# Linear layer with bias and residual on one core: the weight in one load behind the bias, and the last two x loads moved forward in the queue

## Chip, core and metric

The kernel runs on one core of one Trainium2 chip. The metric is device time in microseconds (us). The core's compute engines are called by their short names: PE is TensorE, DVE is VectorE, ACT is ScalarE, POOL is GpSimd. SP is SyncE, which computes nothing here and only issues transfers (DMAs).

## The reference

All arrays are float32.

```python
batch, m, k, n = 16, 512, 1024, 768   # x: batch,m,k  weight: k,n  bias: n  residual, out: batch,m,n
def reference(x, weight, bias, residual):
    return (np.matmul(x, weight) + bias + residual).astype(np.float32)
```

In and out this is 33.6 MB of x, 3.1 MB of weight, 25.2 MB of residual and 25.2 MB of output, 87.05 MB in all.

## The kernel before

x is taken as 8192 rows, split into 8 groups of 1024 rows. A group is 8 tiles of 128 rows, and it is worked on in two halves of 4 tiles. Every partition holds 8 consecutive rows of a group, so a load of a whole group of x moves 32 KB in one piece for each partition, a load of half a group 16 KB, and a residual or an output group 24 KB.

**The engines.** For each half, ACT casts x to bf16 in two steps (L131, semaphore `cast`, 4 casts a group). DVE transposes blocks of 32 x 32 (L161 and L167), and ACT moves half of the transposed blocks to their places (L136). PE multiplies: 64 matmuls for a half (L327), into four buffers in PSUM (`po`). DVE adds the residual while it takes the result out of PSUM (`evacuate`, L173, semaphore `ev`), two tiles at a time, in place in the residual's buffer. POOL adds the bias to the same two tiles (`add_bias`, L222, semaphore `add`), and from there they are stored. The second pair of evacuations of a group stands behind the transposes of the next group's first half on DVE.

At the start POOL casts the weight to bf16 in two halves (L217, semaphore `wc`); PE waits for both (L314). DVE clears `bias_rows` (L175), waits for the bias, and spreads it over all partitions with a shuffle (L178), all of it ahead of its first transposes.

**The buffers.** One array `data` holds everything that is transferred: four slots for residuals (`r_home`, group g in slot g % 4) and two for x (`x_home`: even groups at X0, odd ones at X1). The weight is staged in the slot of residual 3. The residual of group 7 has no slot of its own; it goes where x of group 6 was.

**The queue.** Every DMA is issued by SP, from one list, `ORDER`, written by hand. `x3` is the load of x of group 3, `x0a` and `x0b` are the halves of group 0, `w0` and `w1` the halves of the weight, `r3` the residual of group 3, `st3` the store of group 3, `st4+` the store of groups 4 and 5 in one DMA, `st7a` to `st7c` the store of group 7 in three parts. SP goes through the list in order and, ahead of each DMA, waits for what that DMA needs. A wait holds all that stands behind it in the list:

- an x load of group g > 1 waits until the group two earlier is cast (`cast`, L260);
- `r4`, `r5` and `r6` wait until the store that last used their slot has landed (L275); `r7` waits until x of group 6 is cast (L271);
- a store waits until the bias has been added to its last tiles (L286);
- the bias load waits until DVE has cleared `bias_rows` (L251);
- every load waits for the load before it on the same semaphore to have landed. This is the helper `load_into`:

```python
before = landed.get(name, 0)
landed[name] = before + 16
if before:
    wait(sp, name, before)
```

The residuals r0 to r7 share the semaphore `r`. Whole x loads and first halves share `xa`, second halves share `xb`; for whole loads SP raises `xb` itself (L264 and L273), by an amount that it works out from `ORDER`.

Of the kernel before, what the change touches and what calls it, by code (L numbers as in the profile page):

```python
# [13 lines left out]
G = 8  # L14
B = 4

ORDER = ("x0a w0 bias w1 x0b r0 x1a x1b r1 x2 r2 x3 r3 x4 st0 "
         "st1 r4 x5 r5 st2 x6a x6b r6 x7 r7 st3 st4+ st6 st7a st7b st7c").split()
PARTS = {"": (0, 8), "a": (0, 4), "b": (4, 8)}
LAST_PARTS = {"a": (0, 3), "b": (3, 6), "c": (6, 8)}  # L20
SPLIT = "st7a"
# [3 lines left out]
def shares(name):  # L25
    if name != SPLIT:
        return [slice(0, P)]
    return [slice(APART, P)] + [slice(m, APART, STEP) for m in range(STEP)]


@with_exitstack
def kernel(
    ctx: ExitStack,
    tc: tile.TileContext,
    x: bass.AP,
    weight: bass.AP,
    bias: bass.AP,
    residual: bass.AP,
    out: bass.AP,
):  # L40
    nc = tc.nc
    stored = ctx.enter_context(nc.semaphore("st"))
    late = 16 * sum(len(shares(name)) for name in ORDER if name[:2] == "st" and int(name[2]) > 2)
    nc.scalar.sem_inc(stored, late)
    with tc.tile_critical(name="all", no_gpsimd_drain=True):  # L45
        emit(nc, ctx, x, weight, bias, residual, out, stored, late)
    nc.sync.wait_ge(stored, late)


def emit(nc, es, x, weight, bias, residual, out, stored, late):  # L50
# [5 lines left out]
    R = K // P  # L56
# [5 lines left out]
    sp, act, dve, pool, pe = nc.sync, nc.scalar, nc.vector, nc.gpsimd, nc.tensor  # L62
# [18 lines left out]
    def sem(name):  # L81
        if name not in sems:
            sems[name] = es.enter_context(nc.semaphore(name))
        return sems[name]

    def wait(eng, name, value):
        eng.wait_ge(sem(name), value)  # L87
# [14 lines left out]
    def group(ap, g):  # L102
        return ap[g * G * P:(g + 1) * G * P, :].rearrange("(p j) k -> p j k", p=P)

    def span(start, size):
        return data[:, start:start + size] if isinstance(start, int) else data[:, bass.ds(start, size)]

    def x_home(g):
        return X0 - (g % 2) * X_SLOT

    def x_rows(start, j, n):
        return span(start + j * K, n * K).rearrange("p (t k) -> p t k", k=K)

    def r_home(g):

        return (g % 4) * R_SLOT + ((g + 1) // n_grp) * (X0 - 3 * R_SLOT)

    def r_rows(start, j, n):
        return span(start + j * N, n * N).rearrange("p (j n) -> p j n", n=N)

    w_stage = span(3 * R_SLOT, R * N).rearrange("p (r n) -> p r n", n=N)
    w_rows = weight.rearrange("(p r) n -> p r n", p=P)
# [90 lines left out]

    for h in (0, 1):
        part = slice(h * (R // 2), (h + 1) * (R // 2))
        wait(pool, f"w{h}", 16)
        pool.tensor_copy(out=w_sb[:, part, :], in_=w_stage[:, part, :]).then_inc(sem("wc"), 1)  # L217
    wait(pool, "bb", 1)

# [20 lines left out]
    def load_into(name):  # L240
# [5 lines that stand above are left out]
        return name  # L246

    for name in ORDER:
        into = name
        if name == "bias":  # L250
            wait(sp, "ev", EV0)  # L251
            src, dst = bias[None, :].to_broadcast((P // Q, N)), bias_rows[0:P:Q, :]
        elif name[0] == "w":
            k0 = int(name[1]) * (R // 2)
            src, dst = w_rows[:, k0:k0 + R // 2, :], w_stage[:, k0:k0 + R // 2, :]
        elif name[0] == "x":
            g, part = int(name[1]), name[2:]
            j0, j1 = PARTS[part]
            if g > 1 and part != "b":
                wait(sp, "cast", 2 * (2 * g - 2))  # L260
            if g == 3:
                wait(sp, "wc", 2)
                whole = 16 * sum(n[0] == "x" and len(n) == 2 and int(n[1]) < n_grp - 1 for n in ORDER)
                sp.sem_inc(sem("xb"), whole)  # L264
                landed["xb"] += whole
            into = load_into("xb" if part == "b" else "xa")
            src, dst = group(x2d, g)[:, j0:j1, :], x_rows(x_home(g), j0, j1 - j0)
        elif name[0] == "r":
            g = int(name[1])
            if g == n_grp - 1:  # L270
                wait(sp, "cast", 2 * (2 * g))  # L271
                if f"x{g}" in ORDER:
                    sp.sem_inc(sem("xb"), 16)  # L273
            elif g > 3:
                wait(sp, f"st{g - 4}", 16)  # L275
            into = load_into("r")
            src, dst = group(res2d, g), r_rows(r_home(g), 0, G)
        else:
            g, part = int(name[2]), name[3:]
            n = 2 if part == "+" else 1  # L280
            j0, j1 = (LAST_PARTS if g == n_grp - 1 else PARTS)[part.strip("+")]
            end = (g + n - 1) * G + j1
            if end == n_sub:
                wait(sp, "ev", ev_end)
            else:
                wait(sp, "add", added[(end - 1) | 1])  # L286
            src, dst = r_rows(r_home(g), j0, j1 - j0), group(out2d, g)[:, j0:j1, :]
            if n > 1:
                src = span(r_home(g), n * R_SLOT).rearrange("p (g k) -> p g k", g=n)
                dst = out2d[g * G * P:(g + n) * G * P, :].rearrange(  # L290
                    "(g p j) n -> p g (j n)", g=n, p=P)
            if g > 2:
                into = "st"
        for rows in shares(name):
            sp.dma_start(out=dst[rows] if name == SPLIT else dst,  # L295
                         in_=src[rows] if name == SPLIT else src).then_inc(sem(into), 16)
# [20 lines left out]
    with pe.Fori(0, n_bat):  # L317
        tiles = iter(range(B))
        for i in range(B):
# [5 lines left out]
            for k in range(R):  # L325
                for c, (n0, nl) in enumerate(chunks):
                    ins = pe.add_instruction(mybir.InstMatmult(  # L327
                        name=nc.get_next_instruction_name(),
# [36 lines left out]
```

## Time and profile before

| | before |
|---|---|
| time, median of 3 runs | 209.27 us (209.25 to 209.3) |
| profiled execution | 209.01 us |
| its span, first to last instruction | 207.2 us |
| mean granted PE clock | 0.984 |
| busy: PE, DVE, ACT, POOL | 170.6, 166.3, 144.9, 115.5 us |
| DMA queue, share of 16 engines' span | 98.3% |
| bytes read, written | 61.88 MB, 25.17 MB |
| SP waiting on landed x, residuals, stores | 51.9, 50.8, 24.4 us |

The profile is of one execution. Busy time is that of instructions with work in them; issuing a DMA and waiting count as idle. A DMA has an issue, which takes SP about 0.33 us, and a landing, which is when its semaphore is full. In between it may stand in the queue behind others. Between the span and the time of the profiled execution lie 1.8 us in which nothing of the kernel runs.

### The profile page before, as it was taken

The page shows a single profiled execution, that of the slowest core. Times are in us where ns is not written, and L with a number is a line of the kernel's source. Part 1 is how long each engine was busy: PE and PEld are TensorE (multiplying, and loading weights), DVE is VectorE, ACT ScalarE, POOL GpSimd, SP SyncE. Part 2 cuts the span into 40 slices and gives each one's busy share as a digit, 9 for nine tenths or more (in the row PEclk, how much of TensorE's full clock was granted, in tenths as well). Part 3 has the DMA queues.
Part 4 walks back from the last instruction along what each step waited for, and adds up shares of the span by engine and source line. Part 5 has one row for each costly group of instructions (what it writes and reads, how often), then busy time and mean ns, then how long its engine had stood idle before and what let it go on. Part 6 is the DMA issues. An engine that isn't in the chain of part 4 may idle for free.

```text
span 207.2 us, 2315 instructions
## 1 busy us (share of the span) xinstructions
PE 170.6 (82%) x1024; PEld 50.6 (24%) x512; DVE 166.3 (80%) x180; ACT 144.9 (70%) x162; POOL 115.5 (56%) x38
## 2 busy tenths in 40 slices
PE   0000999989998999999999999699999999999900
PEld 0000222323332333233332322133322222233200
DVE  1068496999889989999899978998999899983510
ACT  2357976997599696979697679888797969730000
POOL 0055007639391939193938484484829391999800
PEclk9999999999999999999999999999999999999985
DMA  6999999999999999999999999999999999999995
GB/s 209 429 431 436 446 427 414 433 433 487 411 405 449 411 455 405 419 441 455 408 427 474 411 427 413 429 440 449 408 465 411 446 399 441 455 408 427 451 399 218
DMA packets 4472, 87.05 MB, mean 420 GB/s; under 512 B 500, under 2 KB 500, under 8 KB 632
## 3 DMA queue, kind: packets, MB, share of 16 engines
q1 hardware_dynamic: 4472, 87.05, 98.3%
HBM read 61.88 MB, written 25.17 MB: 420 GB/s over the span
## 4 chain that ended last, share of the span: by engine, by line
DMA 77%; PE 10%; DVE 4%; issue 2%; ACT 1%; SPq 0%; DVEq 0%; ACTq 0%
DMA data<-in_x_dram 66%; DMA out_dram<-data 12%; PE po L327 10%; DVE xt L167 2%; DVE data L173 1%; ACT xb L131 1%; DVE tq L161 1%; SPq L295 0%; DVEq L98 0%; SPq L87 0%; ACTq L98 0%; SPq L360 0%; SPq L45 0%
## 5 line engine op out<-in xcount | busy, mean ns | idle before, releaser
L327 PE MATMUL po<-w_sb,xt 128*128 128x512 bf16 (+1 forms) x1024 | 170.6, 329 | 25.9 <-DVE xt L167 20.5
L222 POOL TENSOR_TENSOR data<-data,bias_bc 128x1536 f32<-128x1536 f32 x32 | 109.8, 3455 | 68.3 <-DVE data L173 68.2
L136 ACT COPY xt<-tq 32x512 uint32<-32x512 uint32 x128 | 78.9, 617 | 21.3 <-DVE tq L161 18.5
L167 DVE STREAM_TRANSPOSE xt<-xb 32x512 uint32<-32x512 uint32 x128 | 90.1, 704 | 3.9 <-ACT xb L131 1.9
L327 PEld LDWEIGHTS po<-w_sb,xt 128*128 x512 | 50.6, 99 | 145.5 <-issue 143.9
L131 ACT CAST xb<-data 128x2048 bf16 x32 | 64.8, 2076 | 16.1 <-DMA data<-in_x_dram 15.8
L173 DVE TENSOR_TENSOR data<-po,data 128x1536 f32 (+2 forms) x33 | 55.9, 1709 | 12.4 <-PE po L327 11.9
L161 DVE STREAM_TRANSPOSE tq<-xb 128x1024 uint32<-128x1024 uint32 x16 | 19.8, 1236 | 3.5 <-ACT xb L131 3.5
L217 POOL CAST w_sb<-data 128x3072 bf16<-128x3072 f32 x2 | 5.5, 2744 | 12.6 <-DMA data<-in_weight_dram 12.6
L178 DVE LOAD_MASK_SELECT bias_bc<-bias_rows x1 | 0.0, 14 | 10.3 <-DMA bias_rows<-in_bias_dram 10.3
L140 ACT ACT_TABLE_LOAD x1 | 1.3, 1283 | 1.0 <-SPq L45 1.0
L175 DVE MEMSET bias_rows<- 128x768 f32 x1 | 0.7, 698 | 1.2 <-SPq L45 1.2
L178 DVE STREAM_SHUFFLE bias_bc<-bias_rows 128x768 f32<-128x768 f32 x1 | 1.0, 1005 | 0.0
L349 POOL MEMSET const-float32-0.0<- 128x1 f32 x1 | 0.1, 98 | 0.2 <-issue 0.2
L140 ACT COPY warm<-const-float32-0.0 128x1 f32<-128x1 f32 x1 | 0.2, 191 | 0.0
L349 POOL MEMSET const-bfloat16-1.0<- 128x1 bf16 x1 | 0.1, 101 | 0.0
L349 POOL MEMSET const-uint8-127<- 128x1 uint8 x1 | 0.1, 101 | 0.0
L349 POOL MEMSET const-float32-1.0<- 128x1 f32 x1 | 0.1, 98 | 0.0
## 6 DMA issues: line engine op xcount, KB each, us to landing
data<-in_residual_dram SPq DMA_DIRECT2D x8, 3072.0 KB, 17.0
data<-in_x_dram SPq DMA_DIRECT2D x5, 4096.0 KB, 21.8
out_dram<-data SPq DMA_DIRECT2D x5, 3072.0 KB, 24.1
data<-in_x_dram SPq DMA_DIRECT2D x6, 2048.0 KB, 18.6
out_dram<-data SPq DMA_DIRECT2D x1, 6144.0 KB
data<-in_weight_dram SPq DMA_DIRECT2D x2, 1536.0 KB, 11.8
out_dram<-data SPq DMA_DIRECT2D x1, 1152.0 KB
out_dram<-data SPq DMA_DIRECT2D x1, 1008.0 KB
```

What stands on the lines that cost most here:

```text
L131: act.copy(out=xb[:, c], in_=part.rearrange("p t (a j r) -> p t j a r", j=R // 2, r=2)).then_inc(sem("cast"), 1)
L136: act.copy(out=xt[q * Q:(q + 1) * Q, half, :, :, m * Q:(m + 1) * Q], in_=tq[m * Q:(m + 1) * Q, :, :, q]).then_inc(sem("mv"), 1)
L140: act.copy(out=warm[:], in_=nc.const_aps.tensor(0.0, [P, 1], FP32))
L161: dve.transpose(out=tq[:], in_=xb_words(0)).then_inc(sem("tq"), 1)
L167: ins = dve.transpose(out=xt[q * Q:(q + 1) * Q, half, :, :, m * Q:(m + 1) * Q], in_=words[m * Q:(m + 1) * Q])
L173: dve.tensor_add(out=rt, in0=po[:, j % 4:j % 4 + n, :N], in1=rt).then_inc(sem("ev"), 1)
L175: dve.memset(bias_rows[:], 0.0).then_inc(sem("ev"), EV0)
L178: dve.stream_shuffle(out=bias_bc[:], in_=bias_rows[:], mask=[0] * 32).then_inc(sem("bb"), 1)
L217: pool.tensor_copy(out=w_sb[:, part, :], in_=w_stage[:, part, :]).then_inc(sem("wc"), 1)
L222: pool.tensor_add(out=rt, in0=rt, in1=bias_bc[:, None, :].to_broadcast((P, 2, N))).then_inc(sem("add"), 1)
L327: ins = pe.add_instruction(mybir.InstMatmult(name=nc.get_next_instruction_name(), ins=[pe.lower_ap(w_sb[:, k, n0:n0 + nl]), stationary(i, k)],
L349: nc = _bacc.Bacc("TRN2", target_bir_lowering=False, num_devices=1)
```

## The change

`ORDER` is changed in two places. At the start, `w0 bias w1` becomes `bias w`: the bias load goes ahead of the weight, and the weight is one DMA of 24 KB a partition instead of two of 12 KB. POOL still casts it in two halves, but both wait for the one semaphore. Toward the end, `st2 x6a x6b r6 x7 r7` becomes `x6 st2 x7 r6 r7`: x of group 6 is loaded whole and is issued ahead of the store of group 2, and x of group 7 is issued ahead of the residual of group 6. All else follows from the list.

```diff
-ORDER = ("x0a w0 bias w1 x0b r0 x1a x1b r1 x2 r2 x3 r3 x4 st0 "
-         "st1 r4 x5 r5 st2 x6a x6b r6 x7 r7 st3 st4+ st6 st7a st7b st7c").split()
+ORDER = ("x0a bias w x0b r0 x1a x1b r1 x2 r2 x3 r3 x4 st0 "
+         "st1 r4 x5 r5 x6 st2 x7 r6 r7 st3 st4+ st6 st7a st7b st7c").split()
...
     for h in (0, 1):
         part = slice(h * (R // 2), (h + 1) * (R // 2))
-        wait(pool, f"w{h}", 16)
+        wait(pool, "w", 16)
         pool.tensor_copy(out=w_sb[:, part, :], in_=w_stage[:, part, :]).then_inc(sem("wc"), 1)
...
         elif name[0] == "w":
-            k0 = int(name[1]) * (R // 2)
-            src, dst = w_rows[:, k0:k0 + R // 2, :], w_stage[:, k0:k0 + R // 2, :]
+            src, dst = w_rows, w_stage
```

## The prediction

> **What bounds the kernel now.** I read the page first, then the busy time by stretch, then the chain that ended last, then SP's timeline from 110 us on, and at the end the rows of the engines around the three edits.
>
> ```profile
> span 207.2 us, 2315 instructions
> PE 170.6 (82%) x1024; PEld 50.6 (24%) x512; DVE 166.3 (80%) x180; ACT 144.9 (70%) x162; POOL 115.5 (56%) x38
> DMA  6999999999999999999999999999999999999995
> q1 hardware_dynamic: 4472, 87.05, 98.3%
> ```
>
> One queue carries all 87.05 MB, and its packets fill 98.3% of sixteen engines' span. No compute engine is near that. The stretches show where the missing 1.7% is (columns: stretch, length, busy time of PE, PEld, DVE, ACT, POOL, granted clock, DMA share, GB/s).
>
> ```profile
> 1.00:2.00 1.00, 0.00 (x0) 0.00 (x0) 0.70 (x1) 0.96 (x1) 0.00 (x0) 1.00 0.22 49
> 2.00:3.00 1.00, 0.00 (x0) 0.00 (x0) 0.00 (x0) 0.52 (x2) 0.00 (x0) 1.00 1.01 229
> 3.00:4.00 1.00, 0.00 (x0) 0.00 (x0) 0.00 (x0) 0.00 (x0) 0.00 (x0) 1.00 0.81 328
> 100.00:200.00 100.00, 93.13 (x570) 27.68 (x283) 86.64 (x92) 67.94 (x79) 67.06 (x20) 1.00 1.00 430
> 204.00:205.00 1.00, 0.00 (x0) 0.00 (x0) 0.00 (x0) 0.00 (x0) 0.00 (x0) 0.50 0.58 240
> 205.00:206.00 1.00, 0.00 (x0) 0.00 (x0) 0.00 (x0) 0.00 (x0) 0.00 (x0) 0.50 0.24 98
> ```
>
> It is all at the two ends: a ramp of 2 us after the first issue, and a tail in which a few engines finish alone. In between the queue runs at 430 GB/s with a share of 1.00. So the end is (bytes)/(430 GB/s) plus those ends; a change can win next to nothing here, and it loses every stretch in which the queue stands empty. The whole question is whether SP still issues each transfer before the one ahead of it has drained. The chain (start, length) and SP's timeline give issues and landings:
>
> ```profile
> 0.96 7.24 DMA data<-in_x_dram
> 96.48 24.05 DMA data<-in_x_dram
> 120.59 19.59 DMA data<-in_x_dram
> 140.25 21.86 DMA data<-in_x_dram
> ```
>
> ```profile
> 110.87 0.33 SPq L295 DMA_DIRECT2D data<-in_residual_dram  x1
> 111.25 0.42 SPq L295 DMA_DIRECT2D out_dram<-data  x1
> 120.59 0.80 SPq L295 DMA_DIRECT2D data<-in_x_dram  x2
> 135.35 0.33 SPq L295 DMA_DIRECT2D data<-in_residual_dram  x1
> 140.25 0.33 SPq L295 DMA_DIRECT2D data<-in_x_dram  x1
> 155.69 0.33 SPq L295 DMA_DIRECT2D data<-in_residual_dram  x1
> 156.07 5.13 SPq L295 DMA_DIRECT2D out_dram<-data  x2
> ```
>
> The first column of the chain plus the second is a landing: x5 at 120.53, x6a at 140.18, x7 at 162.11. The trace's landing record adds r5 at 127.84, st2 at 135.33, x6b at 145.08, r6 at 152.39, r7 at 169.43. Landings come in the order of issue, a 3 MB transfer 7.3 to 7.5 us behind the one before it, 4 MB 9.7 us, 2 MB 4.9 us: it is first in, first out. Now look at r7, issued at 155.69. It has two waits, for the casts of x6 (15.0 us at line 273, done 155.6) and, through load_into, for the residual before it, r6, which had landed 3.2 us earlier. While SP waited, x7 (issued 140.25) was still moving until 162.11. That one transfer is the cover of r7's wait.
>
> **The change, part by part.**
>
> x6 whole, ahead of st2. x6 waits for x5's landing (120.53) and for x4's casts, so it issues at 120.59 as x6a did. r5 is in flight until 127.84: no gap. x6 then lands at 127.84 + 9.75 = 137.6, and st2, issued right behind it at about 121, at 145.1. x7 waits for x6's landing (137.6) and for x5's casts (129.74 + 4.03 = 133.8): issued at 137.65 with st2 still moving. No gap either.
>
> x7 ahead of r6. x7 lands at 145.1 + 9.75 = 154.9. r6 waits for st2 (145.1) and issues then, with x7 in flight. It lands where x7 landed before, the bytes ahead being the same: 162.1, or 162.0 after the saving below.
>
> r7 behind r6. Here the cover is gone. The cast wait is over at 155.6 as before (ACT's casts of x6 stood behind its own moves, not behind the data: x6a landed 140.18, ACT was free at 140.4). But load_into holds r7 until r6 has landed, and r6 is now the last thing in the queue. st3 and st4+ could go, their adds being done, but they stand behind r7 in SP's program. So at 162.0 the queue is empty, SP wakes, issues r7, and all sixteen engines start from nothing.
>
> The price of a start from nothing is in this trace once, at x0a: 7.24 us from issue to landing for 2.10 MB, which at 430 GB/s take 4.88 us. The rest, 2.36 us, is what a transfer in a backlog hides. With 0.06 us from a landing to SP's next issue (x5 at 120.53, x6a at 120.59) the gap is 2.42 us. The Trainium skill ("DMA: Bandwidth & Descriptors", section on the anatomy of one DMA) puts a fixed cost of about 2.0 us on every DMA, for the GpSimd path; by that the gap would be 2.06 us and the time 0.36 us less than mine.
>
> To this comes the spread of the engines. At r6's landing before, sixteen engines came in from 151.61 to 152.39, mean 151.83: 0.56 us from mean to last, against 0.14 at x0a. r7 waits for the last one, so an ordinary engine loses up to 0.42 us more than x0a's 2.36 contains; the laggard loses none of it. In the tail (205 to 206 us, share 0.24, four to five engines) both kinds are among the last, so 0 to 0.42; I take half, 0.2.
>
> From both sides: x0a may be dear because it was the first of all, with 16 KB packets of 0.9 to 1.45 us against 0.61 later. Without what that slow first packet cost (0.65) and with half of the 1.0 us from issue (0.96) to the first packet (1.97 in the trace's packet record) the gap is 1.3 us. Above, the full spread (0.42) and a restart dearer by one packet's 0.4 us give 3.2. I take 2.6, close to the only row that has such a start.
>
> The weight whole. PE waits for both weight casts (line 314).
>
> ```profile
> 11.99 2.74 POOL L217 CAST w_sb<-data 128x3072 bf16<-128x3072 f32 x1 [11.55 <-DMA data<-in_weight_dram]
> 15.76 2.75 POOL L217 CAST w_sb<-data 128x3072 bf16<-128x3072 f32 x1 [1.02 <-DMA data<-in_weight_dram]
> ```
>
> The first cast now waits for the whole weight, at 15.7; the two end at 15.76 + 2 x 2.75 = 21.26 instead of 18.51, and PE, which started at 20.53 after DVE's transposes, starts at 21.3 to 21.9: 0.8 to 1.4 us later. What hides it is PE's slack and the data of x5:
>
> ```profile
> 122.86 1.25 DVE L161 STREAM_TRANSPOSE tq<-xb 128x1024 uint32<-128x1024 uint32 x1 [0.65 <-ACT xb L131]
> 124.86 5.73 DVE L167 STREAM_TRANSPOSE xt<-xb 32x512 uint32<-32x512 uint32 x8 [0.75 <-ACT xb L131]
> ```
>
> At group 5 DVE waits 0.65 and 0.75 us for casts of data that lands at 120.53, and at group 2 for 0.47 us; there the delay is used up, and from 132.65 on PE keeps its times. No SP wait falls in between: x3, x4 and st0 wait for casts and adds that end 3 us or more ahead of their issue. Without this cover PE would end 1.4 us later than 196.6; st7c, issued at 199.0, still has some 5 us of queue ahead of it. Cost: nothing.
>
> The bias first. It now lands right behind x0a (about 8.4 instead of 12.12), so bias_bc no longer holds DVE's first transposes until 13.05; xt is ready some 2 us earlier, and PE waits for the weight anyway. Its issue (0.68 us) delays w's, with x0a moving until 8.2. Nothing.
>
> Bigger packets. Two DMAs fewer; packets of 16 KB take 38.35 ns per KB and engine, of 12 KB the same, of 24 and 32 KB 38.0 to 38.1. For x6 (256 KB an engine) that is 0.08 us, for w (192 KB) 0.05: 0.13 us won.
>
> r6 later (152.4 to 162.0) is needed by DVE's first evacuation of group 6, which ran at 162.48 behind its own transposes: 0.4 us to spare, and a miss would only reach PE, with the 5 us above. r7 about 2.4 us later, at 171.8, is needed at 183.9.
>
> **Sum.** 2.6 - 0.13 = 2.5 us on the queue's path, which is the end. The profiled execution took 209.01 us (span 207.2 and 1.8 around it), the median is 209.27, 0.26 above. Profiled after: 211.5; median 209.27 + 2.5 = 211.8.
>
> **Rivals.**
>
> The restart is cheap (1.3 us, minus 0.13): 210.4. For it: x0a was the very first transfer. Against: no row shows a quick start. Chance 0.08.
>
> No gap, so not slower: r6 and x7 share the engines instead of queueing, r6 lands before x7 has drained, and r7 is issued under cover. Then 209.27 - 0.13 = 209.1. It decides the case if r6 lands 2.4 us ahead of x7's end. Against it speak the landings in strict order of issue. Chance 0.04.
>
> Each DMA in the backlog has a fixed cost of its own, and two fewer pay for the gap: if x0a's 2.36 us were paid by every transfer, the change would win 2 x 2.36 and lose 2.6, giving 207.2. The Trainium skill ("DMA: Bandwidth & Descriptors", rules for kernel authors) says to coalesce many small transfers, which points that way. Against it: x6a and x6b took 4.9 us each in the queue, x4 whole 9.7, so the second DMA cost 0.1 us at most. Chance 0.02.
>
> A dearer gap (over 3.2 us), or r6 so late that DVE and PE run into the tail as well: 213. Chance 0.03.
>
> **Numbers.** The forecast has 0.83, from 210.9 to 212.6. The range takes in part of the cheap restart and the upper bound: 210.6 to 212.7. About 0.2% (0.42 us) is what a measurement of this kernel can tell from no change. Slower by more: the forecast, the cheap and the dear gap, 0.94; within: 0.04; faster: 0.02.
>
> **What would show it.** In SP's timeline r7's issue at about 162.1, 0.06 us behind r6's landing, waiting on the residual and no longer on line 273; st3 and st4+ within 1 us behind it; a dip of DMA share to near 0 for about 1 us at 162 to 164, and nowhere else; PE starting near 21.6 but at 132.7 again for group 5, and ending at 196.6; the span near 209.7. I am wrong if r7 is issued while packets still move, or if the share dips at a second place (x7 at 137.6, r6 at 145.1).

## The result and the profile after

The changed kernel takes 213.06 us (median of 5 runs, 212.76 to 213.13) against 209.27 us: 1.0179 times as long, 95% interval 1.0168 to 1.0191. That is 3.8 us more; the prediction had 2.5 us more and a range that ended at 212.7. The profiled execution took 212.76 us, with a span of 211.0. Two executions far from all others, one of the kernel before (658 us) and one of the later kernel r7_own_sem (1044 us), are left out of the ratios below.

The page's answers to the lines shown of before:

```profile
span 211.0 us, 2313 instructions
PE 170.8 (81%) x1024; PEld 50.5 (24%) x512; DVE 166.5 (79%) x180; ACT 145.0 (69%) x162; POOL 115.4 (55%) x38
DMA  6999999999999999999999999999998899999995
q1 hardware_dynamic: 4184, 87.05, 97.4%
```

The engines work as long as before. The queue's share fell from 98.3% to 97.4%, and the row of slices has two eights near three quarters of the span, where it had nines. SP's timeline in that place:

```profile
162.14 0.33 SPq L294 DMA_DIRECT2D data<-in_residual_dram  x1
162.52 0.90 SPq L294 DMA_DIRECT2D out_dram<-data  x2
```

r7 is issued at 162.14, when r6 lands (162.12 in the landing record), and not at 155.69 as before; st3 and st4+ follow at once. What the queue does meanwhile (columns: stretch, length, busy time of PE, PEld, DVE, ACT, POOL, granted clock, DMA share, GB/s):

```profile
160.00:161.00 1.00, 1.00 (x8) 0.29 (x3) 0.97 (x3) 0.98 (x2) 0.71 (x1) 1.00 0.69 295
161.00:162.00 1.00, 1.00 (x8) 0.29 (x3) 0.99 (x2) 0.95 (x3) 0.00 (x0) 1.00 0.01 0
162.00:163.00 1.00, 1.00 (x8) 0.29 (x3) 0.81 (x2) 1.00 (x1) 0.00 (x0) 1.00 0.00 0
163.00:164.00 1.00, 1.00 (x7) 0.29 (x3) 1.00 (x1) 1.00 (x2) 0.00 (x0) 1.00 1.77 393
164.00:165.00 1.00, 1.00 (x7) 0.29 (x3) 0.55 (x2) 1.00 (x1) 0.60 (x1) 1.00 0.63 270
...
170.00:171.00 1.00, 1.00 (x8) 0.30 (x4) 0.99 (x2) 0.95 (x2) 1.00 (x1) 1.00 1.60 393
171.00:172.00 1.00, 1.00 (x8) 0.32 (x4) 0.99 (x2) 0.97 (x2) 0.27 (x1) 1.00 0.11 25
```

The kernel before, at 170 us:

```profile
170.00:171.00 1.00, 1.00 (x8) 0.32 (x4) 0.99 (x2) 0.97 (x2) 1.00 (x1) 1.00 1.03 442
```

A packet is counted whole where it begins, so a share above 1 with no more than 430 GB/s beside it means packets that take long. The dip in the first four rows is the empty queue that was forecast: in the trace's packet record no packet with data begins between 160.74 and 163.09 us. The last two rows were not forecast: at 170 us the packets are slow again. The last two packets of r7 on each engine take up to 1.85 us instead of 0.912, together 17.2 us more over 16 engines, which is 1.08 us an engine. They are the last before st3. r7 lands at 173.28 instead of 169.43, 3.85 us later, and the end of the span moves by the same 3.8.

### The profile page after: what moved, and what is told of

The parts are those of the page before. It is cut to its first block, busy times and chain, and to the rows that moved or that the text cites. A ratio compares the mean times of both kernels' runs of the same rounds, so it can differ in the third digit from the quotient of the medians.

```text
span 211.0 us, 2313 instructions
## 1 busy us (share of the span) xinstructions
PE 170.8 (81%) x1024; PEld 50.5 (24%) x512; DVE 166.5 (79%) x180; ACT 145.0 (69%) x162; POOL 115.4 (55%) x38
## 3 DMA queue, kind: packets, MB, share of 16 engines
q1 hardware_dynamic: 4184, 87.05, 97.4%
## 4 chain that ended last, share of the span: by engine, by line
DMA 64%; PE 18%; DVE 6%; ACT 2%; issue 2%; SPq 0%; DVEq 0%; ACTq 0%
DMA data<-in_x_dram 53%; PE po L326 18%; DMA out_dram<-data 11%; DVE xt L167 4%; DVE data L173 2%; ACT xb L131 1%; ACT xt L136 1%; DVE tq L161 1%; SPq L294 0%; DVEq L98 0%; SPq L87 0%; ACTq L98 0%; SPq L359 0%; SPq L45 0%
```

## The experiments

An extra time of slow packets below is always worked out in this way: what the packets took beyond 38.1 ns per KB, summed, over 16 engines. Times stand against runs of the kernel before on the same chip (medians 209.1 to 209.27). The three kernels with one timed run, st3_late, gap_x2 and gap_store, have no interval.

**One order at a time: swap_only and no_swap.**

```diff
 # swap_only, from the kernel before
-st2 x6a x6b r6 x7 r7 st3
+st2 x6a x6b x7 r6 r7 st3
 # no_swap, from the changed kernel
-x6 st2 x7 r6 r7 st3
+st2 x6 r6 x7 r7 st3
```

> The kernel before with one edit: x7 ahead of r6; w0, w1, x6a, x6b stay as they were. Theory: the whole 3.8 us come from r7, which waits for r6 with the queue empty, so 213.1 us, an empty queue at 161 to 163, and slow packets again at the end of r7 (about 1.1 us). Rival, the other two edits carry the part that my sum lacks (1.3 us): then 211.8 and no slow packets at the end of r7.

> The changed kernel with its loads back in the old order (st2, x6, r6, x7, r7), x6 and the weight still whole. Theory: no wait is uncovered, so 209.1 us (209.27 less 0.13 for the bigger packets), no empty queue between 4 and 204 us. Rival, the whole loads cost something of their own: up to 210.6.

swap_only: 213.34 us (1.0194, interval 1.0176 to 1.0213), no share at 162 us, slow packets at the end of r7 (1.16 us). Its profile is of the longest of its four executions, 214.44 us. Putting x7 ahead of r6 is enough for the whole loss.

no_swap: 211.87 us (1.0136, 1.0118 to 1.0154), which neither sentence of its expectation covers. It has no empty queue at 162; its trouble is PE (profile of its shortest execution, 211.06 us; timeline: start, length, engine, line, operation, count, idle time before):

```profile
157.21 22.65 PE L326 MATMUL po<-w_sb,xt 128*128 128x512 bf16 x126 [3.30 <-DVE data L173]
180.35 20.97 PE L326 MATMUL po<-w_sb,xt 128*128 128x512 bf16 x126 [0.49 <-DVE data L173]
```

Loaded whole behind st2, x6 lands at 145.13, while half of it was there at 140.19 before. ACT waits 4.54 us for it. Group 6 starts on PE at 157.21 instead of 154.10, group 7 at 180.35 instead of 175.57, and at the end the queue runs out of stores twice:

```profile
197.00:198.00 1.00, 1.00 (x8) 0.29 (x3) 0.92 (x1) 0.00 (x0) 0.39 (x2) 1.00 0.29 123
201.00:202.00 1.00, 0.32 (x2) 0.00 (x0) 0.64 (x1) 0.00 (x0) 0.42 (x1) 1.00 0.39 148
```

So a whole x6 needs its place ahead of st2. In the changed kernel it has that place, and PE starts group 6 at 154.04.

**The wait taken away: r7_own_sem, and covered: st3_first.**

```diff
 # r7_own_sem, from the changed kernel
-into = load_into("r")
+into = load_into("r" if g < n_grp - 1 else "rl")
-wait(pool, "r", 16 * n_grp)
+wait(pool, "rl", 16)
 # ... and ahead of st6, so that DVE's count of "r" comes out
+wait(sp, "rl", 16)
+sp.sem_inc(sem("r"), 16)
 # st3_first, from the changed kernel
-x7 r6 r7 st3 st4+
+x7 r6 st3 r7 st4+
```

> The changed kernel with one wait gone: r7 has a semaphore of its own, so it no longer waits for r6, only for the casts of x6 (155.6), with x7 still moving. Theory (all of the loss is this wait): 209.3 us, no empty queue, no slow packets. Rival (the order itself costs): up to 210.5, as with st3 ahead of r7.

> The changed kernel with st3 issued ahead of r7, so that 3 MB are in flight while r7 waits for r6. Theory: no empty queue, r7 lands near 176.9, still ahead of its use at 183.9; 209.1 us. Rival, the slow packets at 169 to 172 us belong to that time or to r7's meeting with stores and not to the restart: 210.2.

r7_own_sem: 209.11 us, ratio 0.9999 (0.9989 to 1.0009). Order and sizes are those of the changed kernel; only r7 no longer waits for r6.

```profile
162.00:163.00 1.00, 1.00 (x8) 0.29 (x3) 0.85 (x2) 1.00 (x1) 0.00 (x0) 1.00 0.97 418
170.00:171.00 1.00, 1.00 (x8) 0.30 (x4) 0.99 (x2) 0.98 (x2) 1.00 (x1) 1.00 1.09 467
```

Both the empty queue and the slow packets are gone. All of the loss is that one wait.

st3_first: 210.39 us (1.0053, 1.0034 to 1.0071), 1.3 us more than expected. There is no empty queue at 162, and there are no slow packets at 169 to 172 nor where r7 now meets st4+ (176 to 179), so the rival's mechanism is absent, though its time is nearer. The difference lies in the tail: the engine that lags lands r7 1.27 us behind the mean (0.58 in the kernel before) and ends alone, with a last landing at 207.73, when the one before it is at 206.35. Why it lags more in this order stays open.

**What the slow packets belong to: fill_shift, st3_late, gap_loads, gap_x6.** They could belong to the restart, to the moment at which r7 ends, or to the end of any restarted load. Each kernel parts two of these.

```diff
 # fill_shift, from the kernel before: rows of group 3 stored twice
-x6a x6b r6 x7 r7 st3
+x6a x6b r6 fill x7 r7 st3
+elif name == "fill":
+    wait(sp, "add", added[31])
+    src, dst = r_rows(r_home(3), 0, 3), group(out2d, 3)[:, 0:3, :]
 # ... and ahead of st3
+wait(sp, "fill", 16)
 # st3_late, from the changed kernel, ahead of st3
+wait(sp, "r", 16 * n_grp)
 # gap_loads, from the changed kernel
-x6 st2 x7 r6 r7 st3
+x6 st2 r6 x7 r7 st3
 # gap_x6, from st3_first, ahead of x6
+wait(sp, "r", 16 * 6)
```

> The kernel before, with 1.18 MB more to move and no restart: a part of group 3's output is stored a second time between r6 and x7 (2.75 us of queue), so that r7 ends and st3 begins as late as in the changed kernel. Theory (the slow packets at the end of r7 belong to the restart): none here, 212.0 us. Rival (they belong to the moment at which r7 ends, whatever shifted it): slow packets at 170 to 172 us, 213.1 us.

> The changed kernel with a second empty queue made on purpose: st3 waits until r7 has landed. Theory (the last two packets of r7 on each engine are slow because they meet st3's first ones): no slow packets at the end of r7, which lands near 172.2 at the latest instead of 173.3; then a second gap of about 2 us, 214 to 215 us. Rival (the end of a restarted load is slow whatever follows): slow packets at 169.5 to 172 as before.

> The changed kernel with r6 ahead of x7 (x6, st2, r6, x7, r7): r6 waits for st2's landing at 145.1 with nothing behind st2 in the queue, and two loads follow it. Theory (the second stall comes only where a store follows the restarted load): one empty stretch at 144 to 146.5, costing 2.6 to 2.8 us, no slow packets at the end of r6, 211.9 us. Rival (any restart has a second stall at the end of its first transfer): slow packets near 154 too, 213.0 us.

> The order of the kernel with st3 ahead of r7 (no empty queue, 210.4 us), with a restart put elsewhere: x6 waits for r5's landing at 127.8, and st2 stands behind x6. Theory (restart of a load, then a store: a second stall): slow packets at the end of x6 (138 to 140 us), about 1.1 us, and 210.4 + 2.7 + 1.1 = 214.2 us. Rival (the slow packets belong to 169 to 172 us): none at the end of x6, 213.1 us.

fill_shift: 212.31 us (1.0170, 1.0132 to 1.0207). r7 lands at 172.52, against 173.28 in the changed kernel, so its last packets run at the time in question, and none of them is slow:

```profile
170.00:171.00 1.00, 1.00 (x8) 0.32 (x4) 0.97 (x3) 0.97 (x2) 1.00 (x1) 1.00 0.97 418
```

The moment is not the cause.

st3_late: 214.96 us in one run. r7 restarts as in the changed kernel, but its end meets no store:

```profile
170.00:171.00 1.00, 1.00 (x8) 0.29 (x3) 0.99 (x2) 0.98 (x2) 1.00 (x1) 1.00 0.91 393
171.00:172.00 1.00, 1.00 (x7) 0.29 (x3) 0.99 (x2) 0.95 (x3) 0.31 (x1) 1.00 0.01 0
```

No packet is slow there, and r7 lands at 172.08, 1.2 us ahead of the changed kernel. This also gives the first part by itself: from r6's landing (162.16) to r7's 9.92 us, of which 3.15 MB at 430 GB/s are 7.32, so a load's restart costs 2.60 us. The second restart, with a store, costs less: from 172.08 to st3's landing at 180.88 are 8.80 us, so 1.48. Of the load's 2.60 us, 0.80 are its first packets, which take 1.42 to 2.14 us; the store's first packets take 0.97 us at most. The two restarts make 4.1 of the 5.9 us that this kernel loses. The rest arises behind 195 us, among the last stores, and stays open.

gap_loads: 212.90 us (1.0191, 1.0162 to 1.0220), 1.0 us above the theory and close to the rival, and neither had the place: the theory named no slow packets, the rival those at the end of r6. r6 is the restarted load, and nothing is slow at its end; the slow packets stand some 24 us after the restart, where r7 meets st3:

```profile
145.00:146.00 1.00, 1.00 (x8) 0.32 (x4) 1.00 (x2) 0.00 (x0) 1.00 (x1) 1.00 0.00 0
154.00:155.00 1.00, 0.82 (x5) 0.29 (x3) 1.00 (x1) 1.00 (x1) 1.00 (x1) 1.00 1.13 483
171.00:172.00 1.00, 1.00 (x8) 0.32 (x4) 0.99 (x2) 0.95 (x3) 0.26 (x1) 1.00 0.34 98
```

From 169 to 172 us the extra time is 1.04 us an engine, although SP issued r7 at 155.76 and st3 at 156.14, with x7 still moving.

gap_x6: 212.60 us (1.0164, 1.0147 to 1.0181). The restart is at 128 us, the next store, st2, stands behind x6:

```profile
127.00:128.00 1.00, 1.00 (x8) 0.31 (x4) 0.99 (x2) 0.95 (x3) 0.00 (x0) 1.00 0.00 0
138.00:139.00 1.00, 1.00 (x8) 0.30 (x4) 0.97 (x3) 0.98 (x2) 1.00 (x1) 1.00 2.18 524
139.00:140.00 1.00, 1.00 (x8) 0.32 (x4) 0.99 (x2) 0.95 (x3) 0.25 (x1) 1.00 0.00 0
```

The slow packets moved to the end of x6 (1.20 us), and none are left at 169 to 172. x6 lands 3.7 us later than in st3_first (141.19, 137.50). The total rises by 2.2 us only, less than the 3.8 of the theory: the tail of the lagging engine, 1.4 us alone in st3_first, is gone after the restart.

**How long it is remembered: gap_x2 and gap_store.**

```diff
 # gap_x2, from r7_own_sem, ahead of x2
+wait(sp, "r", 16 * 2)
 # gap_store, from st3_first, ahead of st3
+wait(sp, "r", 16 * (n_grp - 1))
```

> The kernel in which r7 has a semaphore of its own (209.1 us, no empty queue), with a restart put early: x2 waits for r1's landing at 45. Five loads follow (x2, r2, x3, r3, x4) before the first store, st0. Theory (a restart is remembered until the first store behind a load, however late): 2.6 us at the restart, and slow packets of about 1 us an engine at the end of x4, near 88 to 91 us, where the other kernels lose 0.1 to 0.4; 212.5 us. Rival (the memory fades within a few loads): no more than 0.4 us at the end of x4, 211.7 us. Neither expects slow packets at the end of r7.

> The kernel with st3 ahead of r7, where st3 now waits for r6's landing at 162.1, so the queue restarts with a store, and r7 and st4+ stand behind it. Theory (what is slow is the first store after a restart that has to follow a load): the store restarts in about 1.5 us, the end of r7 (near 178) shows no slow packets, 210.4 + 1.5 = 211.9 us. Rival (the first meeting of a load with a store behind it, wherever the restart began): slow packets at the end of r7, 213.0 us.

gap_x2: 212.59 us in one run, 0.1 from the theory. The restart is at 45 us; x4 meets st0 after five loads:

```profile
89.00:90.00 1.00, 1.00 (x7) 0.29 (x3) 1.00 (x1) 1.00 (x1) 0.00 (x0) 1.00 2.02 524
90.00:91.00 1.00, 0.51 (x4) 0.10 (x2) 1.00 (x2) 1.00 (x2) 0.41 (x1) 1.00 0.00 0
```

The slow packets come to 0.92 us an engine, more than 40 us after the restart; in the kernel before, the same meeting has 0.11.

gap_store: 212.80 us in one run, nearer to the rival's 213.0 than to the theory's 211.9. Packets are slow where st3 ends and r7 begins (168 to 172 us, 0.9 us an engine) and again where r7 meets st4+ (175 to 179 us, 0.95):

```profile
169.00:170.00 1.00, 1.00 (x8) 0.29 (x3) 0.97 (x3) 0.95 (x3) 1.00 (x1) 1.00 1.60 393
176.00:177.00 1.00, 1.00 (x8) 0.29 (x3) 1.00 (x1) 1.00 (x1) 1.00 (x1) 1.00 1.64 467
```

I had not expected the first of these at all.

## Why the prediction was wrong

**The bound and the place were right.** The queue sets the end, and the one new wait that counts is r7's for r6: issue at 162.14 (forecast 162.1), st3 and st4+ within 1 us, an empty queue at 161 to 163. No gap opened at x7 or r6. r7_own_sem and swap_only show that this wait is the loss.

**The sum's first term was right.** I took 2.6 us for the start from nothing. Three kernels restart a load without slow packets at its end, and there the price is 2.49 (gap_x2), 2.60 (st3_late) and 2.86 us (gap_loads), from landing to landing less the bytes at 430 GB/s. That the 0.2 us for the spread of the engines is right in itself, no run shows. The Trainium skill's fixed cost of about 2.0 us ("DMA: Bandwidth & Descriptors", anatomy of one DMA), given there for the GpSimd path, lies between what a load (2.6) and a store (1.5), both issued by SP, paid here. The part of that page which ties the cost most to HBM as the target does not show in these two numbers: the load, whose target is the core's memory, paid more.

**The step that failed** is the line "The price of a start from nothing is in this trace once, at x0a", as the whole price of the gap. The term was 2.6 us and measured 3.84: r7 landed 11.16 us behind r6, and 7.32 of these are its bytes. Of the 3.84 us, 1.08 stand at the end of r7, where the first store stands behind a restarted stretch of loads; the other 2.76 lie within what a restart alone cost. x0a did not show this second part: the first meeting of a load with a store after it (x4 and st0, at 88 us) has only 0.1 us. My upper bound of 3.2 us was made of pieces of the same single event, so it could not hold a second event either. The missed term is why 213.06 lies above the range.

**Bigger packets**: forecast 0.13 us won. r7_own_sem has them, and stands at 0.9999 with an interval of 0.1% to each side; r6 lands at 162.12, where x7 landed before with the same bytes ahead. A gain of that size is not seen, nor excluded.

**The weight whole**: PE started at 22.33, 1.8 us later, against a forecast of 0.8 to 1.4. The casts ended at 21.25, as forecast; PE began 1.08 us behind them, and not 0 to 0.6. As forecast the delay is used up at group 5 (132.58; before 132.65), by the waits for x5's casts:

```profile
124.80 5.73 DVE L167 STREAM_TRANSPOSE xt<-xb 32x512 uint32<-32x512 uint32 x8 [0.29 <-ACT xb L131]
```

Of the 0.65 and 0.75 us of waiting in front of these transposes 0.29 are left. The cost is nothing, as summed, but with little to spare.

**The cover behind PE was overstated.** I wrote that a later PE has some 5 us of queue to use up. In no_swap PE starts group 7 4.8 us later, and the kernel is 2.7 us slower (1.9 in the profiled execution). It did not matter for this change, whose PE was not late; it was the reason for a wrong expectation later.

**The rivals.** No gap: excluded by the empty queue. A cheap restart: excluded by 2.5 to 2.9 us. A fixed cost that two fewer DMAs save: excluded by r7_own_sem, which has two fewer and takes the same time. A dearer gap, at 0.03, was the case that came; the other half of that rival, DVE and PE running into the tail, did not: PE ended at 196.6. Its 213 had no sum behind it, so that it came close is luck.

## What to carry to other kernels

Where one queue carries everything, go through its issues and ask of each wait what is still moving when it ends; a semaphore shared by a row of loads puts each behind the landing of the last, and a swap of two loads can take the cover away. A queue that ran empty once cost 3.4 to 4.2 us here against the kernel before (gap_x2 and swap_only), not the 2.6 us that the empty stretch and the restart show; against its own parent, st3_first, gap_x6 lost 2.2 us, with the tail of the lagging engine gone as well. A price taken from one row covers what happened in that row. The start of the program priced the restart here, and not what a restart in mid-run leaves for the next meeting of a load with a store, and a range built from that row alone could not hold it.

## What the runs showed of the hardware

After the queue has run empty, the first place where a load meets a store behind it has slow packets: 0.92 to 1.20 us an engine in six kernels, whether that place comes 10 us or more than 40 us after the restart, and whether or not the store was issued under a full queue. It vanishes when the store is held back until the load has landed (st3_late), and later meetings in the same run are clean (r7 and st4+ in gap_x6, 0.06 us). When the restart began with a store, the first change from store to load is slow too (0.9 us). What in the DMA engines keeps this memory, and why the program's own start leaves only 0.1 to 0.4 us of it, no run here shows.
